# A fused short-convolution and mixture-of-experts layer: the order of the first loads and modulation, expert 0's loads, the search steps, expert 2's join and the last scatter

## The chip, the cores and the metric

The kernel runs on one core of one Trainium2 chip. Its time is in device microseconds (us), and a time given for a kernel is the median over its runs. TensorE (PE in the profile) multiplies, VectorE (DVE), ScalarE (ACT) and GpSimd (POOL) work element by element, and SyncE (SP) issues most DMAs. Each engine takes its instructions in the order in which they stand in the program.

## The reference, cut to what matters

One layer (DEPTH = 1, kind 0) over 2048 tokens of 1024 channels; all data are float32.

```python
m_l = (silu_c @ ada_w[i] + ada_b[i])[:, None, :]            # 1024 x 6144
sh1, sc1, g1, sh2, sc2, g2 = jnp.split(m_l, 6, axis=-1)
hl = modulate(rms_norm(lat, norm_g[i, 0]), sh1, sc1)        # x * (1 + scale) + shift
gate_b, gate_c, v = jnp.split(hl @ w_in, 3, axis=-1)        # 1024 x 3072
yl = (gate_b * dwconv_centred(gate_c * v, conv_w)) @ w_out  # 3 taps along the tokens
lat = lat + g1 * yl
h = modulate(rms_norm(lat, norm_g[i, 1]), sh2, sc2)
aff = jax.nn.softmax(h @ w_router, axis=-1)                 # 16 experts
g, idx = lax.top_k(jnp.swapaxes(aff, 1, 2), 256)            # each expert takes 256 tokens
hid = jax.nn.silu(xs @ w_gate) * (xs @ w_up)                # xs = h[idx]; 1024 x 1024 per expert
lat = lat + g2 * scatter_add(idx, (hid @ w_down) * g)
```

## The kernel before

**Products.** Each float32 operand is held as a rounded high part and the rest as a low part (fp32r), and a product is three matmuls: high by high, high by low, low by high. A piece of weights (512 KB) is loaded into a `raw` tile; ScalarE copies it to its high part (`split_high`, L212), VectorE subtracts to get the low part (`split_low`, L222), which frees the buffer and issues the next load. SP issues these loads (L196), in order.

**The head.** The four quarters of 512 tokens are `xq[q]`, four tiles of 128 rows each. `norm_x` scales the rows to unit norm: ScalarE sums the squares (L280), GpSimd makes 1/root of it in two small steps, VectorE multiplies (L393). `to_hl(q, k)` turns channel block k (128 channels) of a quarter on TensorE (four transposes, L398), applies scale `A1` and shift `sh1` on ScalarE twice, once rounded (L401) and once in full, and takes the low part on VectorE; the result is `hl[q, k]`. sh1 and A1 themselves are columns of `silu_c @ ada_w`: `load_ada_cols(k)` loads the 128 columns of block k for the shift and for the scale, with rows of 512 bytes; `ada_cols` lets VectorE sum the eight row blocks, weighted by `s_col`, into two accumulators `acc` of 256 columns (L429); `ada_sum` adds up the partitions by two matmuls of one column (`pcol`, L438), and `ada_fix` makes sh1 and A1 of it on VectorE.

`in_mm` is one step of `hl @ w_in`: nine matmuls of 512 columns (L451, L452, L454) into three banks, for the three channel blocks of gate_b, gate_c and v with the same number `ct`. Eight of them, k = 0 to 7, fill the banks, and `in_out` empties them. The loop of the head runs the pairs ct = 0 and ct = 1 of quarter 0 with a lag of three, `in_mm(pair[0], .., k)` beside `in_mm(pair[1], .., k - 3)`, so 16 in_mm in all; `norm_x(1, b)` stands at k = 6 and the eight `to_hl(1, j)` at k = 7 to 10. Then `constants()` (tables for the routing on GpSimd and VectorE) and the router's load follow, and the loop over `steps` takes up the remaining (ct, quarter) with eight in_mm each. Its first step, `steps[0]`, is quarter 1 with ct = 0.

**Routing and experts.** Which tokens an expert takes is found by a search for a threshold, in steps that are spread over other work: `tick(k)` runs the next step, in which TensorE's `pc` waits for ScalarE's count `hit` (L965 for L959). `pick_oh(e)` and `pick(e)` make the token numbers and issue two gathers `xs` on GpSimd (L1072); `fetch(0, i)` turns expert 0's rows (L1088), `turn` and `join` do it for the other experts. `gate_up(e, fh)` and `down(e, dh)` are the products (matmuls of 256 and of 512 columns), and after `down(e, 1)` two indirect DMAs on GpSimd add the result to the output (L1180). Behind `pick(0)` stand six matmuls `warm` (L1200), whose result nothing reads, and `split_to(first + 3)`, which splits expert 0's first four pieces and issues four more loads.

## Time and profile before

| what | value |
|---|---|
| median of 3 runs (lowest to highest) | 1913.16 us (1910.98 to 1913.17) |
| profiled execution, its own time | 1912.57 us |
| its span in the trace | 1910.8 us |
| its mean granted TensorE clock | 0.983 |
| PE busy | 1836.3 us, 96% of the span |
| DVE busy | 1136.9 us, 60% |
| ACT busy | 823.7 us, 43% |
| POOL busy | 304.4 us, 16% |
| HBM read, written | 300.51 MB, 50.33 MB |

The span is the time between the first and the last instruction or transfer in the trace of one execution; that execution's own time is 1.8 us longer. Busy times are means over stages with different limits: PE's 96% says that the kernel as a whole is bound by TensorE, and what is left to gain lies in the 74 us in which PE was not busy. A granted clock of 1.00 is TensorE's upper level, 2.4 GHz, and 0.50 the lower, 1.2 GHz.

### The profile page before, as it was taken

To read this page: it belongs to the slowest core of one execution; us is meant where nothing else is said; L and a number is where in the kernel's file an instruction comes from. 1 tells how busy PE (TensorE), PEld (TensorE's weight loads), DVE (VectorE), ACT (ScalarE), POOL (GpSimd) and SP (SyncE) were. 2 spreads that over 40 slices of the span, in tenths; PEclk is the share of its full clock that TensorE was granted. 3 is DMA by queue.
4 is the path that set the end of the run, shared out by engine and by line. 5 is a ranking of instruction groups with operands and counts; after the bars stand their busy time and mean duration, and the time that the engine had idled before them with its cause. 6 is when DMAs were issued, how large, how long until landed. Compare 5 with 4: busy or idle time off the path is not lost.

```text
span 1910.8 us, 29082 instructions
## 1 busy us (share of the span) xinstructions
PE 1836.3 (96%) x11568; PEld 1628.8 (85%) x11568; DVE 1136.9 (60%) x1633; ACT 823.7 (43%) x1046; POOL 304.4 (16%) x457
## 2 busy tenths in 40 slices
...
GB/s 281 145 113 146 77 160 61 105 137 143 72 72 190 259 257 257 134 219 201 214 249 216 242 248 249 231 227 266 220 239 236 258 219 241 255 238 236 221 231 89
DMA packets 308316, 375.30 MB, mean 196 GB/s; under 512 B 101788, under 2 KB 183764, under 8 KB 308180
## 3 DMA queue, kind: packets, MB, share of 16 engines
...
q14 instruction: 45, 0.37, 0.1%
HBM read 300.51 MB, written 50.33 MB: 184 GB/s over the span
## 4 chain that ended last, share of the span: by engine, by line
PE 89%; DVE 4%; DMA 3%; issue 1%; ACT 1%; POOL 1%; SPq 1%; POOLq 0%; DVEq 0%; ACTq 0%
PE pm L1131 12%; PE pm L1133 12%; PE pm L1135 12%; PE pm L451 9%; PE pm L452 9%; PE pm L454 9%; PE pm L1156 6%; PE pm L1154 6%; PE pm L1155 6%; PE pm L656 2%; PE pm L657 2%; PE pm L659 2%; DMA hl<-hl 1%; DMA xt<-in_x_dram 1%; PE pt L398 1%
## 5 line engine op out<-in xcount | busy, mean ns | idle before, releaser
L222 DVE TENSOR_TENSOR ws<-raw,ws 128x1024 fp32r<-128x1024 f32 x434 | 515.6, 1221 | 272.4 <-ACT ws L212 272.4
L212 ACT ACTIVATE ws<-raw 128x1024 fp32r<-128x1024 f32 x437 | 441.3, 1051 | 410.7 <-PE pm L1135 326.9
L1131 PE MATMUL pm<-xT,ws 128*128 128x256 f32 x2048 | 568.8, 278 | 0.0
L1133 PE MATMUL pm<-xT,ws 128*128 128x256 f32 x2048 | 567.1, 277 | 1.0 <-DVE xT L1111 0.9
L1135 PE MATMUL pm<-xT,ws 128*128 128x256 f32 x2048 | 566.8, 277 | 0.0
L1133 PEld LDWEIGHTS pm<-xT,ws 128*128 128x128 f32 x2048 | 385.9, 188 | 2.8 <-DVE xT L1111 1.1
L1131 PEld LDWEIGHTS pm<-xT,ws 128*128 128x128 f32 x2048 | 385.3, 188 | 1.7 <-ACT xT L1110 0.3
L1135 PEld LDWEIGHTS pm<-xT,ws 128*128 128x128 f32 x2048 | 385.2, 188 | 0.0
L451 PE MATMUL pm<-hl,ws 128*128 128x512 f32 x768 | 305.9, 398 | 1.0 <-ACT hl L401 1.0
L452 PE MATMUL pm<-hl,ws 128*128 128x512 f32 x768 | 302.0, 393 | 0.0
L454 PE MATMUL pm<-hl,ws 128*128 128x512 f32 x768 | 217.3, 391 | 0.0
L1180 POOL DMA_INDIRECT out_dram<-ot,idx x32 | 108.0, 3376 | 602.9 <-DVE ot L1174 598.8
L1156 PE MATMUL pm<-ws,hT 128*128 128x512 f32 x512 | 201.6, 394 | 0.0
L1154 PE MATMUL pm<-ws,hT 128*128 128x512 f32 x512 | 201.3, 393 | 0.0
L1155 PE MATMUL pm<-ws,hT 128*128 128x512 f32 x512 | 200.2, 391 | 0.0
L451 PEld LDWEIGHTS pm<-hl,ws 128*128 128x128 f32 x768 | 145.9, 190 | 31.9 <-ACT hl L401 1.4
L452 PEld LDWEIGHTS pm<-hl,ws 128*128 128x128 f32 x768 | 145.9, 190 | 30.5 <-issue 1.0
L454 PEld LDWEIGHTS pm<-hl,ws 128*128 128x128 f32 x768 | 145.5, 189 | 30.8
L461 ACT ACTIVATE cs<-pm 128x512 f32<-128x512 f32 x32 | 19.1, 598 | 332.1 <-issue 261.2
L464 DVE TENSOR_TENSOR u<-cs,pm 128x512 f32<-128x512 f32 x32 | 22.5, 703 | 231.3 <-ACT cs L461 231.3
L1156 PEld LDWEIGHTS pm<-ws,hT 128*128 128x128 f32 x512 | 96.2, 188 | 20.4
L1155 PEld LDWEIGHTS pm<-ws,hT 128*128 128x128 f32 x512 | 96.2, 188 | 20.2
(291 smaller groups left out, 1962.2 us busy)
## 6 DMA issues: line engine op xcount, KB each, us to landing
raw<-in_moe_w_gate_dram SPq DMA_DIRECT2D x128, 512.0 KB, 4.8
raw<-in_moe_w_up_dram SPq DMA_DIRECT2D x128, 512.0 KB, 4.2
raw<-in_moe_w_down_dram SPq DMA_DIRECT2D x128, 512.0 KB, 4.7
...
```

What stands on the lines that cost most here:

```text
L212: nc.scalar.activation(t[:, 0], raws[n_high], AF.Copy)
L222: (eng or nc.vector).tensor_sub(t[:, 1, ..., s], raw[..., s], t[:, 0, ..., s].bitcast(F32))
L451: nc.tensor.matmul(ps[m], wh, t[:, 0], start=(k == 0), stop=False)
L452: nc.tensor.matmul(ps[m], wl, t[:, 0], start=False, stop=False)
L454: nc.tensor.matmul(ps[m], W(k, m)[0], t[:, 1], start=False, stop=(k == KD - 1))
L1131: nc.tensor.matmul(o, w[:, 0, j, c0], xT[:, 0, k], start=(k == 0 and f % 2 == 0), stop=False, skip_group_check=True)
L1133: nc.tensor.matmul(o, w[:, 0, j, c0], xT[:, 1, k], start=False, stop=False, skip_group_check=True)
L1135: nc.tensor.matmul(o, w[:, 1, j, c0], xT[:, 0, k], start=False, stop=(k == KD - 1), skip_group_check=True)
L1154: nc.tensor.matmul(ps[s], h, w[:, 0, j], start=(k == 0), stop=False)
L1155: nc.tensor.matmul(ps[s], h, w[:, 1, j], start=False, stop=False)
L1156: nc.tensor.matmul(ps[s], l, w[:, 0, j], start=False, stop=(k == KD - 1))
L1180: st = nc.gpsimd.indirect_dma_start(out=out_rows, out_offset=bass.IndirectOffsetOnAxis(ap=idx_of[e][:, s:s + 1], axis=0), in_=ots[s], in_o ...
```

## The change

In the **head**, quarter 0 of x loads first. ada_w's columns come in four groups of two channel blocks, 256 columns a piece (rows of 1 KB), and w_in's columns of ct = 0 and 1 come together, in four parts by rows, in the same order (`load_w`, `high_w`, `low_w`). The weighted sum has one accumulator of 512 columns; its first product is ScalarE's in groups 1 to 3, and in group 0 TensorE takes the first three row blocks itself, multiplied by `s_col` (`ada_mm`). `ada_fix` runs on ScalarE. `wake(n)` issues transposes that nothing reads. Both pairs run side by side, without a lag, two k in a group. The squares of quarter 0 are shared between ScalarE and VectorE. Quarter 1's norms stand in the last group, its first three `to_hl` there and behind it, and the other five inside steps[0]. `constants()`, the router's rows and the start values of `cnts` move into the loop over steps.

At **expert 0**, `split_to(first + 3)` issues its four loads from GpSimd (`load_by`), behind the gathers, and 14, 8 and 3 warm matmuls stand where six stood. The **search steps** (`tick`) skip the k at which TensorE's order now has something else, and **expert 2's** turn and join come one k and one place earlier. The **last scatter** (expert 15) goes in five parts: two halves after `down(15, 0)`, then a half and two quarters, the quarters as products of their own with 256 columns (`last_down`, `scatter_part`).

```diff
+    load_by = [nc.sync]
...
-        nc.sync.dma_start(t, dram(src, offset, ap))
+        load_by[0].dma_start(t, dram(src, offset, ap))
...
+        def to_hl(q, k):
+            turn_x(q, k)
+            low_x(q, k, scale_x(q, k))
...
+        groups = [(0, 2), (2, 2), (4, 2), (6, 2)]
+
+        def load_ada_cols(g):
+
+
+            k0, n = groups[g]
+            ada_t[g] = []
+            for r in range(0, KD, 2):
+                t = hl_tile([P, 2, 2, n * P], F32)
+                ada_t[g].append(t)
+                for j in range(2):
+                    nc.sync.dma_start(t[:, j], dram(ada_w, (r + j) * P * 6 * D + k0 * P,
+                                                    [[6 * D, P], [D, 2], [1, n * P]]))
...
+        def ada_cols(g, r0, r1):
+
             for r in range(r0, r1):
+                if g not in ada_a:
+                    ada_a[g] = m2("acc")
+                    if g:
+                        nc.scalar.activation(ada_a[g], ada_row(g, r), AF.Copy, scale=s_col[:, r:r + 1])
+                    else:
+                        nc.vector.tensor_scalar(ada_a[g], ada_row(g, r), s_col[:, r:r + 1], None, op0=ALU.mult)
                 else:
+                    nc.vector.scalar_tensor_tensor(ada_a[g], ada_row(g, r), s_col[:, r:r + 1], ada_a[g],
+                                                   op0=ALU.mult, op1=ALU.add)
             if r1 == KD:
+                ada_t.pop(g)
...
+        def ada_mm(g, v, col):
+            n, new = groups[g][1], g not in pcols
+            if new:
+                pcols[g] = tp.tile([P, 2, n], F32, name="pcol", tag="tp")
             for h in range(2):
+                for j in range(n):
+                    c0 = (n * h + j) * P
+                    nc.tensor.matmul(pcols[g][:, h, j:j + 1], v[:, c0:c0 + P], col, start=(new and h + j == 0),
+                                     stop=True, skip_group_check=True)
+
+        def ada_sum(g):
+            ada_mm(g, ada_a.pop(g), ones_f[:, 0:1])
+
+        def ada_fix(g, j):
+            k = groups[g][0] + j
+            s = slice(k, k + 1)
+            nc.scalar.activation(sh1[:, s], pcols[g][:, 0, j:j + 1], AF.Identity, bias=bsh_col[:, s])
+            nc.scalar.activation(A1[:, s], pcols[g][:, 1, j:j + 1], AF.Identity, bias=A0[:, s], scale=g0_col[:, s])
...
+            if ps_ == 0 and ct < 2:
+                return lambda k, m: tuple(w_pair[m, k // 4][:, j, k % 4, ct * P:(ct + 1) * P] for j in range(2))
...
+        def load_w(g):
+            for m in range(3):
+                if g == 0:
+                    w_raw[m, 0] = wpool.tile([P, 4, 2 * P], F32, name="raw", tag="raw", bufs=n_raw)
+                elif g == 2:
+                    w_raw[m, 1] = hl_tile([P, 4, 2 * P], F32) if m else b4("rb", [P, 4, 2 * P])
+                nc.sync.dma_start(w_raw[m, g // 2][:, 2 * (g % 2):2 * (g % 2) + 2],
+                                  dram(w_in, 2 * g * P * 3 * D + m * D, [[3 * D, P], [3 * D * P, 2], [1, 2 * P]]))
...
+        def wake(n):
+            t = mm.tile([P, QT], F32, name="pm", tag="mm")
+            for i in range(n):
+                nc.tensor.transpose(t[:, 0:P], xq[0][0][:, 0:P], identf)
+
+        def mm_pair(i, k):
+            in_mm(pair[i], 0, W_chan(0, i), k)
...
+        load_x(0)
         load_ada_cols(0)
+        load_w(0)
         load_ada_cols(1)
+        load_w(1)
+        vrow, nr = row_cols("v_row", [(ada_b, 0, 16), (norm_g, 0, 8), (conv, 0, 24)], nc.gpsimd)
+        rs = [rstd_of(xq[0][b], m2("sq", D, BF) if b % 2 else junk, nc.vector if b % 2 else None) for b in range(3)]
+        norm_x(0, 0, nc.scalar, rs[0])
+        rs.append(rstd_of(xq[0][3], m2("sq", D, BF), nc.vector))
+        norm_x(0, 1, nc.scalar, rs[1])
+        for b in range(2, 4):
+            norm_x(0, b, None, rs[b])
         vcols = to_cols("v_col", vrow, nr)
         bsh_col, bsc_col, g0_col = vcols[:, 0:8], vcols[:, 8:16], vcols[:, 16:24]
         cw = [vcols[:, 24 + 8 * i:32 + 8 * i] for i in range(3)]
+        A0 = consts.tile([P, 8], F32, name="A0")
+        nc.vector.scalar_tensor_tensor(A0, bsc_col, 1.0, g0_col, op0=ALU.add, op1=ALU.mult)
+        for r in range(3):
+            ada_mm(0, ada_row(0, r), s_col[:, r:r + 1])
+        turn_x(0, 0)
+        ada_cols(0, 3, KD)
+        wake(12)
+        ada_sum(0)
+        high_w(0)
+        for m in range(3):
+            low_w(0, m)
+        wake(8)
         pair = [new_banks() for _ in range(2)]
+        for g in range(4):
+            k = 2 * g
+            more_g = g < 3
+            ada_fix(g, 0)
+            full = scale_x(0, k)
+            ada_fix(g, 1)
+            if g:
+                low_w(g, 1)
+                low_w(g, 2)
+            if more_g:
+                ada_cols(g + 1, 0, 1)
+            low_x(0, k, full)
+            mm_pair(0, k)
+            turn_x(0, k + 1)
+            full = scale_x(0, k + 1)
+            if more_g:
+                ada_cols(g + 1, 1, 5)
+            low_x(0, k + 1, full)
+            mm_pair(1, k)
+            if more_g:
+                turn_x(0, k + 2)
+                high_w(g + 1)
+                ada_cols(g + 1, 5, KD)
+            else:
+                rs = [rstd_of(xq[1][b], junk) for b in range(4)]
                 for b in range(4):
+                    norm_x(1, b, None, rs[b])
+            mm_pair(0, k + 1)
+            if g < 2:
+                load_ada_cols(g + 2)
+                load_w(g + 2)
+            if g == 1:
+                load_x(1)
+            if more_g:
+                ada_sum(g + 1)
+                low_w(g + 1, 0)
+            else:
                 in_out(pair[0], 0, 0)
+                to_hl(1, 0)
+            mm_pair(1, k + 1)
+        to_hl(1, 1)
+        to_hl(1, 2)
+        load_end[0] = len(pieces)
+        load_to(n_done + n_raw - 1)
         pend = (pair[1], 0, 1)
...
+                if (ps_, ct, q) == (0, 0, 1) and k + 3 < KD:
+                    to_hl(1, k + 3)
...
+            if i == 3:
+                before, ones_b, tri, slot_r, step, bias, need, zero1, cnts, aux, same, quick = constants(m2)
+                nc.sync.dma_start(rt, dram(router, 0, [[E, P], [E * P, KD], [1, E]]))
+                nc.scalar.activation(rts[:, :, 0], rt, AF.Copy)
+                nc.vector.tensor_sub(rts[:, :, 1], rt, rts[:, :, 0].bitcast(F32))
...
+    def last_down(ps, product):
+
+        ots = ot_of[E - 1]
+
+        def finish(s, o, c0, n):
+            nc.vector.scalar_tensor_tensor(ots[s][:, c0:c0 + n], o, gate_of[E - 1][:, s:s + 1], g2b[:, c0:c0 + n],
+                                           op0=ALU.mult, op1=ALU.mult)
+            scatter_part(s, c0, n)
+
+        for k in range(KD):
+            product(0, k)
+        finish(0, ps[0], H, H)
+        for i in range(2):
+            c = slice(i * CAP, (i + 1) * CAP)
+            o = mm.tile([P, CAP], F32, name="pm", tag="mm")
+            for k in range(KD):
+                w, j, t = ws_of[w_moe[2, E - 1, 1, k // 2]], k % 2, slice(P, 2 * P)
+                h, l = (hT_of[E - 1][k // 4][:, n, k % 4, t] for n in range(2))
+                nc.tensor.matmul(o, h, w[:, 0, j, c], start=(k == 0), stop=False)
+                nc.tensor.matmul(o, h, w[:, 1, j, c], start=False, stop=False)
+                nc.tensor.matmul(o, l, w[:, 0, j, c], start=False, stop=(k == KD - 1))
+            finish(1, o, H + i * CAP, CAP)
...
+        if (e, dh) == (E - 1, 0):
+            index_parts([(0, 0, H), (1, 0, H)])
+            index_parts([(0, H, H), (1, H, CAP), (1, H + CAP, CAP)])
+            for s in range(2):
+                scatter_part(s, 0, H)
...
-    for i in range(6):
-        nc.tensor.matmul(warm, same, ws_of[first][:, 0, 0], start=(i == 0), stop=(i == 6 - 1))
+
+    def keep_warm(n):
+        for i in range(n):
+            nc.tensor.matmul(warm, same, ws_of[first][:, 0, 0], start=(i == 0), stop=(i == n - 1))
+
+    keep_warm(14)
+    split_high(first + 4)
+    load_by[0] = nc.gpsimd
     split_to(first + 3)
+    load_by[0] = nc.sync
     for i in (0, 2, 1, 3):
         fetch(0, i, mm)
+        if i > 1:
+            keep_warm(8 if i == 2 else 3)
     for e in range(E):
         if e == 0:
             gate_up(0, 0, lambda k: pick_oh(1) if k == 1 else pick(1) if k == 3 else
                     (tick(k), turn(1, 0) if k == 7 else None) if k in (2, 4, 5, 6, 7) else None)
             gate_up(0, 1, lambda k: join(1, k // 2 - 2) if k in (4, 6) else
-                    (tick(k), turn(1, 1) if k == 1 else None) if k < 4 else None)
+                    turn(1, 1) if k == 1 else tick(k) if k in (0, 2, 3, 5) else None)
             continue
         if e == 1:
-            gate_up(1, 0, lambda k: tick(k) if k else None)
+            gate_up(1, 0, lambda k: tick(k) if k not in (0, 2) else None)
             down(0, 0, tick)
             for _ in rounds:
                 pass
             pick_oh(2)
-            gate_up(1, 1, lambda k: pick(2) if k == 1 else turn(2, k - 5) if k in (5, 6) else None)
+            gate_up(1, 1, lambda k: pick(2) if k == 1 else turn(2, k - 4) if k in (4, 5) else
+                    join(2, 0) if k == 7 else None)
```

Where instructions stand now, at three places. First SP's queue at the start of the program, as it was before; `raw` with 128x4x128 is half a piece of w_in for ct = 0:

```order
L75 DMA c_row<-in_c_dram 8x128
L414 DMA hl<-in_ada_w_dram 128x4x128 x4
L384 DMA xt<-in_x_dram 128x1024 x4
L75 DMA v_row<-in_ada_b_dram 16x128
L75 DMA v_row<-in_norm_g_dram 8x128
L75 DMA v_row<-in_sc_conv_dram 24x128
L240 DMA raw<-in_sc_w_in_dram 128x4x128 x3
L414 DMA hl<-in_ada_w_dram 128x4x128 x4
L240 DMA raw<-in_sc_w_in_dram 128x4x128 x3
L414 DMA hl<-in_ada_w_dram 128x4x128 x4
L196 DMA raw<-in_sc_w_in_dram 128x8x128 x3
L414 DMA hl<-in_ada_w_dram 128x4x128 x20
```

And SP's queue at the same place in the change:

```order
L75 DMA c_row<-in_c_dram 8x128
L363 DMA xt<-in_x_dram 128x1024 x4
L407 DMA hl<-in_ada_w_dram 128x2x256 x8
L535 DMA raw<-in_sc_w_in_dram 128x2x256 x3
L407 DMA hl<-in_ada_w_dram 128x2x256 x8
L535 DMA raw<-in_sc_w_in_dram 128x2x256 x3
L407 DMA hl<-in_ada_w_dram 128x2x256 x8
L535 DMA rb<-in_sc_w_in_dram 128x2x256
L535 DMA hl<-in_sc_w_in_dram 128x2x256 x2
L407 DMA hl<-in_ada_w_dram 128x2x256 x8
```

x moved ahead of ada_w, each group's ada_w and w_in alternate, and the small `v_row` loads left this queue.

Second TensorE around quarter 1's first transposes. Before, they stood behind an in_mm of pair[1] whose operand `hl_407` had long been made, with another such in_mm behind them (`xt_467` to `xt_473` are quarter 1's tiles):

```order
L454 MATMUL pm_203<-hl_407,ws_296 128x512
L454 MATMUL pm_204<-hl_407,ws_332 128x512
L454 MATMUL pm_205<-hl_407,ws_335 128x512
L398 MATMUL pt_627<-identf_79,xt_467 128x128
L398 MATMUL pt_627<-identf_79,xt_469 128x128
L398 MATMUL pt_627<-identf_79,xt_471 128x128
L398 MATMUL pt_627<-identf_79,xt_473 128x128
```

In the change they stand between in_mm(0, 7) and in_mm(1, 7), the last two of the four groups (`xt_437` to `xt_443` are quarter 1's tiles):

```order
L458 MATMUL pm_252<-hl_566,ws_404 128x512
L458 MATMUL pm_253<-hl_566,ws_406 128x512
L458 MATMUL pm_254<-hl_566,ws_408 128x512
L379 MATMUL pt_625<-identf_79,xt_437 128x128
L379 MATMUL pt_625<-identf_79,xt_439 128x128
L379 MATMUL pt_625<-identf_79,xt_441 128x128
L379 MATMUL pt_625<-identf_79,xt_443 128x128
L455 MATMUL pm_255<-hl_566,ws_404 128x512
```

Both of those in_mm read `hl_566`, the last block of quarter 0; the transposes moved from four in_mm ahead of the end of the pairs to one ahead of it.

Third GpSimd's queue from expert 0's gathers on, before:

```order
L824 CAST aux<-ex 128x16
L1072 DMA xs<-hscr,idx 128x1024 x2
L1072 DMA xs<-hhalf,idx 128x2048 x4
L1180 DMA out_dram<-ot,idx 2048x1024
L1179 MEMSET spacer 1x1
```

And in the change:

```order
L884 CAST aux<-ex 128x16
L1132 DMA xs<-hscr,idx 128x1024 x2
L196 DMA raw<-in_moe_w_up_dram 128x2x512
L196 DMA raw<-in_moe_w_gate_dram 128x2x512
L196 DMA raw<-in_moe_w_up_dram 128x2x512
L196 DMA raw<-in_moe_w_gate_dram 128x2x512
L1132 DMA xs<-hhalf,idx 128x2048 x4
L1288 DMA out_dram<-ot,idx 2048x1024
```

Four weight loads, which SP issued, now stand on GpSimd's queue behind expert 0's two gathers.

## Rows read from the trace of the kernel before

**Rows 1.** Windows: from:to, length, busy us (PE PEld DVE ACT POOL), PEclk, DMA, GB/s.

```profile
19.59:51.81 32.22, 20.14 (x69) 15.35 (x70) 30.65 (x62) 11.14 (x15) 12.28 (x7) 0.74 1.16 300
...
78.36:100.99 22.63, 22.63 (x110) 18.79 (x109) 10.70 (x30) 9.50 (x16) 8.42 (x79) 1.00 0.04 13
100.99:780.00 679.01, 676.49 (x3177) 557.41 (x3175) 334.82 (x447) 220.17 (x298) 105.03 (x238) 1.00 0.49 149
...
798.00:836.70 38.70, 15.38 (x66) 11.84 (x67) 27.57 (x117) 18.59 (x42) 3.34 (x2) 0.50 0.42 150
836.70:1901.96 1065.26, 1061.01 (x7935) 993.08 (x7934) 691.55 (x884) 535.20 (x625) 149.50 (x77) 1.00 0.77 230
```

**Rows 2.** Waits of PE from 0 to 101 us: total us, times, longest.

```profile
PE pcol L438 <- DVE acc L431: 19.1, 5, 7.0
```

**Rows 3.** Timeline of PE in the head: start us, length us, engine, line, operation.

```profile
36.12 0.63 PE L451 MATMUL pm<-hl,ws 128*128 128x512 f32 x1
36.55 0.63 PE L452 MATMUL pm<-hl,ws 128*128 128x512 f32 x1
...
80.52 1.03 PE L398 MATMUL pt<-identf,xt 128*128 128x128 f32 x8
...
98.79 0.39 PE L451 MATMUL pm<-hl,ws 128*128 128x512 f32 x1
...
100.15 0.84 PE L454 MATMUL pm<-hl,ws 128*128 128x512 f32 x3
100.83 0.39 PE L451 MATMUL pm<-hl,ws 128*128 128x512 f32 x1
```

**Rows 4.** DMA from 0 to 120 us, in 40 slices of 3 us.

```profile
GB/s 5 255 319 405 321 291 290 290 286 294 292 291 288 287 294 290 359 394 205 0 0 38 283 320 326 250 99 6 0 0 0 0 0 0 95 87 106 290 336 145
```

**Rows 5.** Groups by form, 0 to 101 us: busy us, mean ns, idle before.

```profile
L401 ACT ACTIVATE hl<-pt,sh,A 128x512 fp32r<-128x512 f32 x16 | 12.5, 780 | 31.9 <-PE pt L398 21.1 <-DVE A L445 7.8 <-issue 2.9
L250 ACT ACTIVATE ws<-raw 128x512 fp32r<-128x512 f32 x6 | 3.8, 628 | 1.9 <-DMA raw<-in_sc_w_in_dram 1.8
L469 DVE SCALAR_TENSOR_TENSOR y<-u,v_col,y 128x512 f32<-128x512 f32 x2 | 1.5, 751 | 1.8 <-ACT y L468 1.8
L251 DVE TENSOR_TENSOR ws<-raw,ws 128x512 fp32r<-128x512 f32 x2 | 1.3, 678 | 0.0
```

**Rows 6.** Timeline of quarter 1's norms: first square, last norm.

```profile
66.22 1.05 ACT L280 ACTIVATE junk<-xt 128x1024 bf16<-128x1024 f32 x1
...
73.05 0.75 DVE L393 TENSOR_SCALAR xt<-xt,rstd 128x1024 f32<-128x1024 f32 x1 [0.71 <-POOL rstd L283]
```

**Rows 7.** Expert 0's gathers `xs`: PE's waits, timeline, issue to landing us.

```profile
PE pt L1088 <- DMA xs<-hscr,idx: 6.6, 2, 4.1
...
822.55 1.80 POOL L1072 DMA_INDIRECT xs<-hscr,idx  x1 [0.30 <-issue]
...
824.69 0.37 SPq L196 DMA_DIRECT2D raw<-in_moe_w_gate_dram  x1
...
830.77 0.48 PE L1088 MATMUL pt<-identf,xs 128*128 128x128 f32 x1 [2.48 <-DMA xs<-hscr,idx]
...
DMA to landing us min/median/max: 5.6/7.4/9.1
```

**Rows 8.** Waits of PE from 836.7 to 1000 us: total us, times, longest.

```profile
PE pc L965 <- ACT hit L959: 2.5, 2, 1.3
PE pm L1133 <- DVE xT L1111: 0.9, 1, 0.9
```

**Rows 9.** The end: timeline; GB/s in 40 slices of 0.21 us from 1902.5 us.

```profile
1901.56 0.40 PE L1156 MATMUL pm<-ws,hT 128*128 128x512 f32 x1
...
1903.02 1.57 POOL L1180 DMA_INDIRECT out_dram<-ot,idx  x1 [3.91 <-DVE ot L1174]
...
GB/s 158 20 0 0 0 0 0 0 0 0 0 0 118 197 0 59 138 178 118 158 217 197 178 257 197 178 257 59 20 0 0 0 0 0 0 0 0 0 0 0
```

**Rows 10.** The scatters: issue ns min/median/max, first and last start.

```profile
L1180 POOL DMA_INDIRECT out_dram<-ot,idx x32: 1552/1620/5977, 957.8 to 1903.0; - x32
```

192 lines of the change are left out of this document (62 added, 130 removed).

## Prediction

> **What bounds the kernel now.** I read the table of stretches first [rows 1]. TensorE is busy in 676.5 of 679.0 us from 101 to 780 us and in 1061.0 of 1065.3 us from 836.7 us to its last matmul; there nothing but its own work sets the end, and the change leaves that work alone. TensorE loses time in three places: the head up to 101 us (20.1 of 32.2 us busy from 19.6 to 51.8), the routing (15.4 of 38.7 us from 798 to 836.7), and what comes behind the last matmul.
>
> In the head its waits [rows 2] name one thing: five waits, 19.1 us together, of `pcol` (ada_sum) for `acc`, VectorE's sums over ada_w's rows. The timeline [rows 3] gives the rest. At 36.1 us a matmul of 512 columns starts 0.43 us behind the one before it (the lower level, 1.2 GHz; the granted clock is 0.74 in this stretch), so that one `in_mm`, 9 matmuls, takes 3.85 us. At 99 us one in_mm starts 2.04 us behind the other (2.4 GHz). The 24th in_mm, the last of steps[0], ends at 100.99 us: the mark against which I measure the head. The DMA row [rows 4] shows loads at about 290 GB/s from 15 to 45 us, where nearly all have rows of 512 bytes (128 columns), and some 400 GB/s where x's 4 KB rows move.
>
> **The change part by part.**
>
> *Head, start.* x (2.1 MB), group 0 of ada_w (2.1 MB) and its share of w_in (0.8 MB) come first. The flow begins near 3 us [rows 4]; x at 400 GB/s takes 5.2 us; the other 2.9 MB have 1 KB rows, whose rate no row shows: at 290 and 400 GB/s they take 10.0 and 7.2 us, and I take 350 (8.3), since 1 KB lies between the two. So w_in's part lands near 17 us. A copy to high parts (0.63), the fix on ScalarE and the scaling (0.78) follow [rows 5]: the first in_mm starts between 18 and 21 us. I take 19.6, which happens to be its start before.
>
> *Head, the four groups.* TensorE's work to the end of the 16th in_mm: 16 x 2.04 = 32.6; seven sets of four transposes at 0.5 (eight take 1.03 [rows 3]), 3.5; three sums of four one-column matmuls, an estimate of 0.35 each, under a set of transposes. That is 37.1 us, some 9.7 in a group. VectorE's work in a group: three low parts of weights and two of hl at 0.68, seven sums of 512 columns at 0.75 [rows 5]: 3.4 + 5.3 = 8.7 us, less than TensorE's. ScalarE's: three copies and a product at 0.63, four scalings at 0.78, four small ones at about 0.2: 6.4. A group's loads (2.9 MB) take 8.3 us at 350 GB/s and 10 at 290; even at 290 the last of w_in lands at 3 + 5.2 + 39.7 = 48 us, before group 3 starts (19.6 + 2.7 + 3 x 9.7 = 51). So TensorE becomes the bound, and the rate matters little. Its clock: before, the first four in_mm ran at the lower level, 1.8 us longer each. Behind the 20 transposes of wake() I take one and a half of them, 2.7 us (bounds 0 and 7.2). Group 3's work would then end at 19.6 + 37.1 + 2.7 = 59.4 us.
>
> *Head, x of quarter 1.* Here the change adds a wait. ScalarE squares the four tiles of quarter 1 behind scale_x(0, 7), and TensorE has to_hl(1, 0), which needs all four, ahead of the 16th in_mm. Before, the chain from the first square (66.22) to the end of the last norm (73.05 + 0.75) took 7.6 us [rows 6], GpSimd's small steps and VectorE's norms in turn, and stood beside in_mm that did not need it. From the end of turn_x(0, 7): 1.55 of scaling + 7.6 = 9.1 us, and TensorE has two in_mm to do meanwhile, 4.1. It waits 5.0 us; in_mm(1, 7), the next transposes, and in_out(pair[0]), which must empty the banks that steps[0] writes, are queued behind.
>
> *Head, sum.* 59.4 + 5.0 + 1.5 (three sets of transposes) + steps[0] with eight in_mm and five sets (18.8) = 84.7; 1.3 for a fall of the clock in that wait (bounds 0 and 3.5: the in_mm and three sets behind it at half speed) gives 86.0. Against 100.99: **-15.0** (bounds: -9, with all four low-clock in_mm and waits for VectorE of half a us in each group, and -20, with the new wait hidden).
>
> On that wait the Trainium skill (TensorE: Matmul & The Clock Gate, "HAM oscillation") says that a TensorE that waits for data between bursts goes back to the lower clock and starts each burst slow. By it the fall costs the full 3.5, and the head would gain 12.8. The granted 0.74 of [rows 1], where TensorE waited again and again, agrees with the rule's direction.
>
> *Constants, router rows, cnts.* They move into steps 3 and 5, into the stretch in which TensorE is busy 676.5 of 679.0 us and VectorE 335; nothing waits for them before 798 us: 0. Without that cover the bound is the 8.4 us that GpSimd was busy from 78 to 101 us [rows 1].
>
> *Expert 0.* In the routing TensorE waits 6.6 us for the two gathers `xs` [rows 7]. The second is issued from 822.55 to 824.35 and used first at 830.77; four weight loads of 512 KB, the last issued at 824.69 by SP, run beside it. They now stand behind both gathers on GpSimd's queue. The fastest gather took 5.6 us from issue to landing [rows 7]; so would the second, landing at 828.2, 2.5 us earlier (bounds 0 and 3). The clock: until 836.7 us it was granted 0.50 [rows 1], so of some four us of gate_up's matmuls two are lost. 14 + 8 + 3 warm matmuls are to keep it up; but the 8 stand ahead of fetch(0, 1), and at the lower level they take 8 x 0.43 = 3.4 us and eat the earlier gather. Between a gain of 4.5 and one of 0 I take **-3.5**.
>
> *Ticks and expert 2's join.* Two waits of `pc` for ScalarE's hit counts, 2.5 us, and one of 0.9 for expert 2's xT [rows 8]. Ticks next to them are skipped, and join(2, 0) comes a step earlier: of 3.4 us I take **-2.0** (bounds -3.4 and +1, if a wait only moves to another tick).
>
> *Last scatter.* Behind the last matmul (ends 1901.96): VectorE's product of 512 columns (0.75 us by the like of it in [rows 5]), the issue from 1903.02 to 1904.59, data until about 1908.7, the end at 1910.8 [rows 9]. The last piece is now a quarter, 128 x 256: VectorE 0.4, the same issue, and 0.9 of data for 3.5. TensorE's work is the same in matmuls of 256 columns, which gate_up uses throughout. **-2.9** (bounds -3.2, and -1.5 if the issues of the last three pieces queue up on GpSimd).
>
> *Sum.* -15.0 - 3.5 - 2.0 - 2.9 = -23.4: a span of 1887.4 for 1910.8. The profiled execution took 1912.57, so 1889.2; the median of the runs is 0.6 above it, and I say **1889.5 us**. Its own range, from bounds that can go together, is 1884 to 1895 us.
>
> **The rivals.** Less than 0.2% (3.8 us) is about what a measurement of this kernel can't tell from no change.
>
> *The clock stays low through the groups.* If hand-offs leave holes in each group, twelve of the 16 in_mm run at 3.85 us: 22 us more, of which 2.7 are counted; in return the wait for quarter 1 shrinks by 3.6 and no clock is left to fall (1.3). About +14: 1904. For it: before, four in_mm in 32 us ran so. Against: the groups have 9.7 us of TensorE's work in 9.7. 0.10.
>
> *VectorE's sums still end last.* If its 8.7 us stretch to 13 by waits for ScalarE, three groups wait 4 us each, like the five waits of before: 1901.5. Against: seven sums of 512 columns do what 18 instructions of 256 did. 0.07.
>
> *The four loads starve on GpSimd.* Its indirect issues took 1.62 us at the median and up to 5.98 [rows 10]. Four at 6.0 from 824.4 us end at 848.4; the fourth lands some 4 us later and its split ends near 855, where gate_up's second half, 22 us behind the first, wants it at about 851; with the load before it TensorE would wait some 8 us: 1897.5. Nearest row: the median. 0.08. The Trainium skill (SBUF — State Buffer, "SBUF: two separate sides") speaks for this rival: the descriptors of a DMA that GpSimd issues are written by GpSimd itself, some VectorE instructions shut it out of the port for that, and the page advises against that queue beside them.
>
> *All goes well.* No fall of the clock, the wait hidden, the gathers' full 4.5: 1883. 0.12.
>
> *Slower than before.* The mechanism is the head's loads. The other parts gain 8.4, so it turns slower if the head ends after 109.4: group 3 then begins near 74 us, and w_in's last part (13.6 MB in all) lands at 72, under 200 GB/s on the way. No steady slice of these loads shows less than 286 [rows 4]. 0.03. *No difference*: the groups wait as long as before and the rest moves within its bounds. 0.02.
>
> **How the numbers follow.** The main case has 0.58, the rivals what is given. Faster by over 0.2%: 0.95; within: 0.02; slower: 0.03. The range for 8 in 10 takes the main case, the starving loads and the good case: 1883 to 1898.
>
> **What would show it.** The 24th in_mm ends at 86 us (under 82 or over 92, and the head's term is wrong). Waits of `pcol` for `acc` fall from 19.1 us to under 3; a wait of about 5 us of quarter 1's transposes for VectorE's norm appears near 60 us. The granted clock is 1.00 from 25 us on but for a dip behind that wait. gate_up(0, 0) starts 2 to 3 us earlier as seen from pick(0), at 2.4 GHz, and 6 us lie behind the last matmul. The prediction fails if matmuls run 0.43 us apart beyond 30 us, or if quarter 1's transposes don't wait.

## The result and the profile after

The changed kernel takes 1897.13 us (median of 5 runs, 1896.77 to 1903.16) where the kernel before takes 1913.0 in the same comparison: ratio 0.9928, 95% interval 0.9914 to 0.9942. That is faster, as forecast, but by less than the 23.7 us that were forecast: 1897.13 lies 7.6 us above 1889.5 and 0.9 below the end of the range, and the ratio times the median shown before (0.9928 x 1913.16 = 1899.4) lies 1.4 beyond that end. A third or more of the forecast gain did not come. The five runs of the changed kernel lie up to 6.4 us apart, so that a difference of some 2 us between two profiled executions says little by itself. The profiled execution took 1897.13 us, its span is 1895.3 and its mean granted clock 0.990.

The table of stretches of the kernel after (columns as in [rows 1], to which it answers):

```profile
22.70:61.38 38.68, 38.52 (x189) 31.06 (x187) 27.07 (x39) 22.75 (x46) 1.00 (x3) 1.00 0.98 307
61.38:66.13 4.75, 1.12 (x5) 0.55 (x5) 2.61 (x5) 2.51 (x5) 3.46 (x7) 0.93 0.70 242
66.13:69.73 3.60, 3.60 (x12) 2.84 (x13) 2.68 (x6) 2.06 (x3) 0.00 (x0) 0.61 0.00 0
69.73:89.34 19.61, 19.61 (x102) 16.35 (x100) 8.11 (x13) 11.21 (x17) 2.27 (x6) 1.00 0.07 28
89.34:577.32 487.98, 487.98 (x2170) 401.06 (x2168) 201.41 (x270) 115.48 (x156) 61.44 (x203) 1.00 0.35 112
577.32:786.50 209.18, 201.93 (x1087) 166.05 (x1087) 147.82 (x223) 111.79 (x160) 56.80 (x126) 0.99 0.80 230
```

The reader is to see three things. From the first in_mm (22.70) to the end of the 15th (61.38) TensorE now stands still for 0.16 us, where [rows 1] had 12 us of holes in 19.59 to 51.81. Then comes a hole, 61.38 to 66.13, and behind it a stretch at a granted clock of 0.61. And the stretch from the last in_mm (577.32) to the search's first `pS` (786.50) takes 209.18 us for the same 1087 matmuls that took this in the kernel before:

```profile
588.98:796.03 207.05, 200.39 (x1087) 165.40 (x1086) 147.55 (x223) 111.51 (x160) 56.23 (x126) 1.00 0.82 233
```

So something was given back in a stage whose work the change leaves alone. The waits of TensorE up to 90 us, after ([rows 2] had 19.1 us for `acc`):

```profile
PE prow L81 <- DMA v_row<-in_sc_conv_dram: 5.3, 1, 5.3
PE pt L379 <- DVE xt L372: 3.6, 4, 1.1
PE prow L81 <- DMA c_row<-in_c_dram: 2.9, 1, 2.9
PE pcol L437 <- DMA hl<-in_ada_w_dram: 1.9, 1, 1.9
```

The waits for `acc` are gone; quarter 1's transposes wait for VectorE's norms. The timeline of TensorE ahead of the first in_mm, after ([rows 3]):

```profile
10.97 5.25 PE L437 MATMUL pcol<-s_col,hl 128*128 128x1 f32 x24 [1.94 <-DMA hl<-in_ada_w_dram]
16.09 1.09 PE L379 MATMUL pt<-identf,xt 128*128 128x128 f32 x4
16.97 2.77 PE L555 MATMUL pm<-identf,xt 128*128 128x128 f32 x12
19.53 1.71 PE L437 MATMUL pcol<-ones_f,acc 128*128 128x1 f32 x8
21.10 1.95 PE L555 MATMUL pm<-identf,xt 128*128 128x128 f32 x8
22.70 0.78 PE L455 MATMUL pm<-hl,ws 128*128 128x512 f32 x1
```

TensorE's own queue fills this: the 12 one-column matmuls of `ada_mm`, each of which the trace shows as two records of 0.22 us, so 24; four transposes; the 12 transposes of `wake(12)`; and the sum of group 0 (four such matmuls, eight records), all in turn. The sum starts at 19.53, though VectorE's `acc`, which it adds up, is done at 17.85.

Marks read from the timelines (matmul ends and starts) cut every kernel into the same stages. "Head" ends with the 24th in_mm, "in_mm" with the 256th, "routing" with the first `pS`, "search" with the start of `pick(0)`'s last `pi`, "expert 0" with gate_up(0, 0), "ticks" with gate_up(2, 0), "steady" with the last matmul, and "tail" is what lies behind it. Times in us of the profiled executions:

| kernel | first in_mm | head ends | in_mm | routing | search | expert 0 | ticks | steady | tail |
|---|---|---|---|---|---|---|---|---|---|
| before | 19.59 | 100.99 | 487.99 | 207.05 | 23.26 | 38.80 | 119.30 | 924.57 | 8.84 |
| after | 22.70 | 89.34 | 487.97 | 209.18 | 23.53 | 34.85 | 119.49 | 924.46 | 6.48 |
| difference | +3.11 | -11.65 | -0.02 | +2.13 | +0.27 | -3.95 | +0.19 | -0.11 | -2.36 |
| rest_only | 20.51 | 100.62 | 487.98 | 207.50 | 23.27 | 34.64 | 118.47 | 924.46 | 6.76 |
| x1late | 20.91 | 87.27 | 487.94 | 211.40 | 23.54 | 35.18 | 118.55 | 924.46 | 6.76 |
| wake | 20.83 | 87.45 | 487.97 | 212.45 | 23.52 | 34.87 | 121.32 | 924.46 | 6.75 |
| x1early | 21.55 | 82.54 | 487.97 | 210.33 | 23.53 | 34.67 | 121.31 | 924.46 | 6.70 |
| tile_only | 20.67 | 83.55 | 502.94 | 212.83 | 23.60 | 35.27 | 121.43 | 924.46 | 6.72 |

The differences from the head's on add up to -15.5, the difference of the spans.

### The profile page after: what moved, and what is told of

It is laid out like the page before. It is cut to its first block, busy times and chain, and to the rows that moved or that the text cites. A ratio compares the mean times of both kernels' runs of the same rounds, so it can differ in the third digit from the quotient of the medians.

```text
span 1895.3 us, 29225 instructions
## 1 busy us (share of the span) xinstructions
PE 1843.0 (97%) x11655; PEld 1636.0 (86%) x11655; DVE 1122.3 (59%) x1586; ACT 829.4 (44%) x1066; POOL 295.6 (16%) x459
## 4 chain that ended last, share of the span: by engine, by line
PE 86%; DVE 4%; DMA 2%; issue 2%; ACT 2%; SPq 0%; POOL 0%; POOLq 0%; DVEq 0%; ACTq 0%
PE pm L1191 12%; PE pm L1193 12%; PE pm L1195 12%; PE pm L455 8%; PE pm L456 8%; PE pm L458 8%; PE pm L1260 6%; PE pm L1258 6%; PE pm L1259 6%; PE pm L716 2%; PE pm L719 2%; PE pm L717 2%; DMA xt<-in_x_dram 1%; DVE ws L222 1%; PE pt L379 1%
## 5 line engine op out<-in xcount | busy, mean ns | idle before, releaser
L1260 PE MATMUL pm<-ws,hT 128*128 128x512 f32 x504 | 198.4, 394 | 0.0
L1258 PE MATMUL pm<-ws,hT 128*128 128x512 f32 x504 | 198.3, 393 | 0.0
L1259 PE MATMUL pm<-ws,hT 128*128 128x512 f32 x504 | 197.1, 391 | 0.0
L465 ACT ACTIVATE cs<-pm 128x512 f32<-128x512 f32 x32 | 19.1, 598 | 316.7 <-issue 234.9
```

The source lines that it names most:

```text
L1258: nc.tensor.matmul(ps[s], h, w[:, 0, j], start=(k == 0), stop=False)
L1259: nc.tensor.matmul(ps[s], h, w[:, 1, j], start=False, stop=False)
L1260: nc.tensor.matmul(ps[s], l, w[:, 0, j], start=False, stop=(k == KD - 1))
```

## The experiments

**Theories.** The main one has two parts. The shortfall in the head is the chain to the first in_mm and the wait for quarter 1; the 2 us in the routing come from the head's new length, which shifts TensorE's fetches of its own code against the loads of `vscr` (the gated product, which `out_split` loads back from DRAM and ScalarE copies to its high part, L645 before, L705 after). The rivals: the routing's loss comes from what was moved into the loop over steps, or from the new order itself; and the waits in the head hide one behind the other, so that removing one gives nothing.

**rest_only**: the kernel before, with the change at expert 0, the search steps, expert 2's join and the last scatter, and the old head.

> The kernel before with the parts at expert 0, the search steps, expert 2's join and the last scatter, without the new head and without the moved constants. Theory: the parts add up, and these are worth +3.9 (expert 0), -0.2 (search steps and join) and +2.3 (tail): 6.0 us, some 1907.0. The stage of the router then takes what it takes in other runs of before. Rival (the new head costs 2.1 us in the router's stage): 6.0 here as well, but 207.0 us in that stage here and 209 in every kernel with the new head. Rival (the parts at the experts only work behind the new head): under 4 us.

Measured: 1905.6 us (7 runs), ratio 0.9968 (0.9956 to 0.9979). The routing takes 207.50, as before; a second profile of the kernel before (before_again, one run, 1911.12 us) has 207.41. So the tail and expert 0 bring some 6 us by themselves, and the routing's loss comes with the new head or with what moved into the loop, both of which are left out here.

**x1late**: quarter 1's first transposes one in_mm later.

```diff
-                to_hl(1, 0)
             mm_pair(1, k + 1)
+        to_hl(1, 0)
```

> The change with quarter 1's first transposes behind the 16th in_mm, in place of ahead of it. In the change TensorE ends the 15th at 61.38 and starts the 16th at 66.13, and runs that at half rate (3.60 us). Theory (TensorE waits in order for the last norm, and the wait drops its clock): the 16th fills 2.0 of the wait at full rate, the transposes still wait until about 66, and the 24th in_mm ends 2.0 to 3.3 us earlier, at 86.0 to 87.3. Rival (the wait only moves: steps[0] needs the last norm anyway, and the clock falls in the shorter wait too): the gain is 2.0 less what the slower transposes and in_mm lose, 0.5 to 1 us, at 88.3 to 88.8.

Measured: 1900.66 us (4 runs), 0.9943 (0.9926 to 0.9959). From the end of the 15th in_mm to the head's end it takes 28.11 us, after 27.96: nothing gained, and the theory falls here (that the head ends at 87.27, inside its forecast, is due to the start at 20.91). Its timeline behind the 16th in_mm:

```profile
64.42 0.72 ACT L472 ACTIVATE y<-u,v_col 128x512 f32<-128x512 f32 x1 [2.66 <-DVE u L468]
65.05 0.76 ACT L384 ACTIVATE hl<-pt,sh,A 128x512 fp32r<-128x512 f32 x1
...
66.53 1.11 PE L379 MATMUL pt<-identf,xt 128*128 128x128 f32 x4 [1.98 <-ACT full L385]
```

Now in_out's product `y` stands ahead of the scaling on ScalarE, waits 2.66 us for VectorE's `u`, which stands behind the norms, and TensorE waits for the scaling. The late thing is the chain of norms; moving its user only chooses the queue in which the wait stands.

**x1early**: the chain starts earlier instead. The squares of tiles 0 and 1 go to the end of group 2, those of tiles 2 and 3 behind ada_fix in group 3, and the norms follow the low parts there.

```diff
+            if g == 3:
+                rs += [rstd_of(xq[1][b], junk) for b in range(2, 4)]
...
+            for b in range(2, 4 if g == 3 else 2):
+                norm_x(1, b, None, rs[b])
...
+                if g == 2:
+                    rs = [rstd_of(xq[1][b], junk) for b in range(2)]
```

> The change with quarter 1's norms earlier: the squares of two tiles at the end of the third group and of two at the start of the fourth, the norms between the low parts there; the order of the transposes is the change's. From the end of the 15th in_mm to that of the 24th the change takes 27.96 us (29.40 in two kernels with the same head), and moving the transposes behind the 16th in_mm left 28.11. Theory (the last norm, at 65.94, sets the start of the 16th, and the wait for it drops the clock): the chain ends before the 15th in_mm does, no wait and no fall are left, and the stretch takes 22.3 to 24.5. Rival 1 (in_out of the first pair stands ahead of quarter 1's scaling on ScalarE and its banks are those that steps[0] writes, so the wait only moves there): 25.5 to 27. Rival 2 (the squares delay ScalarE in the groups): the 15th in_mm ends over 1 us later as counted from the first one's start (38.68 in the change).

Measured: 1891.63 us (4 runs, 1890.41 to 1893.32), 0.9885 (0.987 to 0.99). This version beats both kernels and has the lowest median of the study. The stretches from the end of the 15th in_mm, of x1early:

```profile
59.81:62.33 2.52, 2.52 (x15) 2.08 (x14) 1.23 (x2) 1.71 (x4) 0.00 (x0) 1.00 0.90 309
62.33:82.54 20.21, 19.84 (x102) 16.34 (x100) 9.74 (x17) 11.87 (x19) 2.84 (x6) 1.00 0.11 43
```

No hole, no fall of the clock, 22.73 us instead of 27.96: the wait and what follows from it were worth 5.2 us.

Part of that is lost again: its ticks take 121.31 us, 1.8 more than after, with the same instructions. The place is expert 2's start, behind two waits for its turned rows (0.8 and 0.9 us), first after, then x1early:

```profile
942.50:946.10 3.60, 3.60 (x32) 3.60 (x33) 3.60 (x4) 2.41 (x3) 0.00 (x0) 1.00 0.45 141
```
```profile
936.98:940.58 3.60, 3.60 (x19) 3.60 (x19) 3.60 (x4) 2.28 (x3) 0.00 (x0) 0.53 0.53 167
```

The granted clock falls to 0.53, and 19 matmuls run where after has 32. The same fall stands in wake, best3, tile_only and sp_loads, whose ticks take 121.2 to 122.0 us.

**wake**: `wake(12)` removed.

> The change without the 12 transposes of wake ahead of the first sum over partitions (the other 8 stay behind it). Theory: VectorE's acc of group 0 is done at 17.85, but TensorE's sum of it starts at 19.53, behind those transposes; fix, scaling and in_mm follow it in a chain of 3.2 us. Without them the first in_mm starts at 21.0 to 21.4 in place of 22.70 and the 24th ends 1.3 to 1.7 earlier, near 87.8. Rival (the transposes bring the clock up): more in_mm run at half rate, 1.8 us longer each; with one more the gain is gone, with two the 24th ends at 91.

Measured: 1900.34 us (4 runs), 0.9942 (0.9925 to 0.9958). From the end of VectorE's `acc` to the first in_mm it takes 3.38 us instead of 4.84, so the 12 transposes cost 1.5 on that chain in after; with them gone the sum waits 0.77 us for `acc`, so the 24 records ahead of them are not what it waits for. But x1late, which has the transposes, needs 3.42 us for the same chain. There the sum takes 0.95 us, where it took 1.71 in after and 1.86 in wake:

```profile
18.55 0.95 PE L437 MATMUL pcol<-ones_f,acc 128*128 128x1 f32 x8
```

Behind it the matmuls of the first in_mm start 0.23 us apart from the second on in x1late, while in after the first four start 0.43 or more apart. That is TensorE at half its speed, although the granted clock is shown as 1.00 for both. So the transposes pay for themselves in some executions and not in others. The six kernels with the changed kernel's whole head have their first in_mm between 21.0 and 23.0, and the routing of wake (212.45) took more than its start gave: some 10 us into it the granted clock is 0.66 over 5 us, in x1late too.

**sp_loads** (expert 0's four loads back on SP), **warm6** (six warm matmuls, as before) and **old_ticks** (before's places of the search steps), each alone:

```diff
-    load_by[0] = nc.gpsimd
...
-    load_by[0] = nc.sync
```
```diff
-    keep_warm(14)
+    keep_warm(6)
...
-        if i > 1:
-            keep_warm(8 if i == 2 else 3)
```
```diff
-                    turn(1, 1) if k == 1 else tick(k) if k in (0, 2, 3, 5) else None)
+                    (tick(k), turn(1, 1) if k == 1 else None) if k < 4 else None)
...
-            gate_up(1, 0, lambda k: tick(k) if k not in (0, 2) else None)
+            gate_up(1, 0, lambda k: tick(k) if k else None)
```

> The change with expert 0's four loads issued by SP again, nothing else undone. From the last matmul of pick(0) to the end of gate_up(0, 0) the kernels of before take 38.65 to 38.80 us, the change 34.85, rest_only 34.64. Theory (the four loads run beside the second gather and delay it by 2 to 2.5 us; the warm matmuls hold the clock, worth the rest): 36.5 to 37.4. Rival 1 (the warm matmuls are all of it): 34.9. Rival 2 (both are needed, since the clock falls in the longer wait): 38.5.

> The change with 6 warm matmuls behind pick(0) and none between the fetches, as before. Theory (the clock is half of the gain at expert 0): gate_up(0, 0) starts at the same place but at half rate for some 4 us, so that the stretch from pick(0) to its end takes 36.5 to 37 in place of 34.85. Rival 1 (the earlier gathers alone keep the clock up): 34.6 to 34.9, or less, since 11 matmuls fall away. Rival 2 (the 8 between the fetches cost what they bring): 34.9 to 35.5 with a slow start but an earlier last fetch.

> The change with the search steps where they stood before, expert 2's turn and join as in the change. From the end of gate_up(0, 0) to that of gate_up(2, 0) the kernels of before take 118.60 and 119.30 us, the change 119.49, others with its steps 118.5 to 119.0 where the clock does not fall. Theory (a skipped step is made up later, so that the search ends later and pick(2) waits for VectorE instead): the two waits of pc of 1.2 us each come back, the waits of pick(2) go, and the stretch takes 118.3 to 119.3. Rival 1 (the new places gain the 2 us that was forecast, and the earlier join loses them): 120.5 or more. Rival 2 (the old places are better): 117.5 or less.

Measured, one run and one profile each: 1902.58, 1900.56 and 1897.1 us; their expert 0 took 37.06, 36.62 and 35.00, after 34.85. So the order of the loads is worth 2.2 us and the warm matmuls 1.8. The first stretch of gate_up(0, 0), after, warm6 and before:

```profile
821.24:825.40 4.16, 4.01 (x34) 3.73 (x33) 4.16 (x5) 3.21 (x4) 0.00 (x0) 1.00 0.73 264
```
```profile
821.86:826.00 4.14, 4.00 (x20) 3.70 (x20) 3.98 (x5) 3.55 (x4) 0.00 (x0) 0.56 0.66 256
```
```profile
832.57:836.70 4.13, 3.99 (x18) 3.69 (x18) 3.71 (x5) 3.92 (x5) 0.00 (x0) 0.50 0.08 9
```

34 matmuls against 20 and 18 in the same time: that is the clock. The ticks of old_ticks take 119.09 us, after 119.49; where the clock does not fall, that stage lies between 118.5 and 120.2 in all kernels. TensorE's waits there, first after, then old_ticks:

```profile
PE pm L1193 <- DVE xT L1171: 1.7, 2, 0.9
PE pi L1121 <- DVE oh L1113: 1.3, 4, 0.3
PE pm L1191 <- ACT xT L1170: 0.6, 1, 0.6
...
PE pc L1025 <- ACT hit L1019: 0.4, 1, 0.4
```
```profile
PE pc L1025 <- ACT hit L1019: 2.1, 2, 1.2
PE pm L1193 <- DVE xT L1171: 0.9, 1, 0.9
```

The wait for the hit counts did go, 2.1 to 0.4, and came back as waits for expert 2's turned rows and for `oh`, since the search ends later and pick(2) stands close behind it.

**after_shift, before_shift, before_shift2**: 64, 48 and 36 matmuls of one column whose result nothing reads, early in the head, which move all later code of TensorE by as many places (and add the tile `zb` that they read).

```diff
+        zb = m2("zb", P, BF)
+        nc.gpsimd.memset(zb, 0.0)
+        dummy = mm.tile([P, QT], F32, name="pm", tag="mm")
+        for i in range(64):
+            nc.tensor.matmul(dummy[:, 0:1], zb, zb[:, 0:1], start=True, stop=True, skip_group_check=True)
```

> The change with 64 more matmuls of one column (and 64 weight loads) on TensorE while it waits for the first data; nothing reads their result. From the last in_mm to pS (the router's stage) before, its second trace and rest_only take 207.05 to 207.50 us, the three kernels with the new head 209.18, 211.40 and 212.45. In these three a 16 KB fetch on the instruction queue starts 8 to 11.5 us ahead of the last in_mm's end, where w_out's last loads and the first loads of vscr run; in the other three it starts 31 us ahead and 2 us behind. Theory (that fetch shares DMA engines with the vscr loads, which land some 0.6 us late, TensorE waits for them, and the chain behind keeps late): the extra instructions move the fetch by half of its period, to 20 to 25 us ahead, and the stage takes 207.3 within 0.5. Rival 1 (the new head slows the stage by something else, buffers or moved constants): 209 to 213 as before the shift. Rival 2 (the clock at the start): the head's end moves too, by over 1 us, but the stage does not.

> The kernel before with 48 such matmuls of one column at the start, where TensorE waits for the first data. They move the 16 KB fetch that stands 2 us behind the last in_mm to some 9 us ahead of it, where it stands in the kernels with the new head. Theory (the fetch delays the vscr loads): the router's stage takes 208.3 to 212 us in place of 207.05 to 207.50, the head changes little. Rival (it is the new head or the moved constants): 207.0 to 207.5.

> The kernel before with 36 matmuls of one column at the start. With 48 the code fetch fell 12.4 us ahead of the last in_mm's end, and the router's stage took 207.93 us against 207.05 to 207.50. With 36 it should fall 6 to 9 us ahead, beside the vscr loads themselves. Theory (the fetch delays them): 208.3 to 212. Rival (the new head slows that stage by something else; 207.93 was within the scatter): 207.0 to 207.6.

Measured: 1900.52 (4 runs), 1913.74 (10 runs, ratio 1.0012, 1.0002 to 1.0022) and 1913.24 us (one run). The routing: 207.85, 207.93 and 209.98. after_shift's head ends 4 us later, 3.2 of them because the first of these matmuls waits for GpSimd's zeroing until 13.38 us. The DMA view of the 12 us ahead of the last in_mm's end, in a second profile of the kernel before (routing 207.41) and in before_shift2 (209.98), queue, packets, MB, share:

```profile
q1 hardware_dynamic: 2512, 2.62, 72.2%
q0 software_dynamic: 80, 0.26, 5.9%
q14 instruction: 1, 0.01, 0.2%
```
```profile
q1 hardware_dynamic: 2509, 2.62, 75.2%
q0 software_dynamic: 80, 0.26, 6.3%
q8 instruction: 1, 0.02, 0.6%
q14 instruction: 1, 0.01, 0.2%
```

In before_shift2 a block of TensorE's code (q8; it moves with the extra matmuls) comes in 1.6 us ahead of the first issue for `vscr`, beside the last loads of w_out. ScalarE's copy of what `vscr` brings, in the kernel before and in before_shift2 (last in_mm's end: 588.98 and 587.63), starts 1.66 and 0.85 us ahead of the last in_mm's end:

```profile
587.32 1.06 ACT L645 ACTIVATE hl<-hl 128x1024 fp32r<-128x1024 f32 x1 [9.81 <-DMA hl<-vscr]
```
```profile
586.78 1.06 ACT L650 ACTIVATE hl<-hl 128x1024 fp32r<-128x1024 f32 x1 [10.62 <-DMA hl<-vscr]
```

With the old head and nothing but these extra matmuls and their tile, the routing takes 209.98 where the block falls 9.4 us ahead of that end; in after it falls 11.3 us ahead. The Trainium skill (Runtime: NRT & Kernel Launch, "Instruction fetch mechanics") says that code comes in blocks of 16 KiB by a DMA queue of the engine's own and that the cost of a block's boundary is mostly hidden. The blocks are there in the trace; here one beside other loads went with a copy that starts 0.8 us later against the mark, against that "hidden", in one execution. But its position doesn't settle the 2 us: with 48 matmuls the block falls 12.4 us ahead and the routing takes 207.93.

Nor does most of the loss arise at the mark. The routing has the same matmuls in all kernels, so each can be timed from the last in_mm's end. Two of them, in the kernel before (588.98) and in old_pad (575.68; described below, it has the changed kernel's code but for one tile's size):

```profile
595.65 1.96 PE L843 MATMUL pl<-rt,st 128*128 128x16 f32 x16 [0.25 <-ACT st L840]
...
766.76 0.66 PE L739 MATMUL pt<-identf,u 128*128 128x128 f32 x4 [0.17 <-DVE hl L744]
```
```profile
582.25 1.96 PE L903 MATMUL pl<-rt,st 128*128 128x16 f32 x16 [0.25 <-ACT st L900]
...
755.22 0.66 PE L799 MATMUL pt<-identf,u 128*128 128x128 f32 x4 [0.91 <-DVE hl L804]
```

The first starts 6.67 us behind the mark in the kernel before, 7.12 in after, 7.49 in before_shift2 and 6.57 in old_pad; the second 177.8, 179.3, 180.7 and 179.5. So old_pad, with no delay at the mark, loses 1.8 us all the same (208.83), and after has 0.45 us there of its 2.13. Another half us of after's is the clock at the end: in the last 5 us of the routing it is granted 0.58, where the kernel before has 0.97.

**best3 and best4**: x1early without `wake(12)`, and that with 64 such matmuls that read the constant `identf`, so that no tile is added.

> The change with quarter 1's norms early and without the 12 transposes ahead of the first sum; no matmuls added. Theory (both edits add up): the first in_mm starts near 21 us, the 24th ends at 81 to 82.5 (x1early: 82.54 with its start at 21.55). The code fetch then falls some 8 us ahead of the last in_mm's end, as in the kernel without the 12 transposes, so the router's stage takes 210 to 212.5, and the profiled execution 1890.5 to 1893. Matmuls of the middle stand 226.7 ns apart. Rival (the kernel with all three edits was slow through one of these two): 234 ns apart, 1906 or more.

> The same with the 64 matmuls of one column at the start, which read the identity matrix and no tile of their own. In the kernel with three edits (its matmuls read a tile of the pool m2, zeroed by VectorE) all matmuls of 512 columns up to the experts stood 234.3 ns apart in place of 226.7, and the middle took 15 us more. Theory for that (the extra tile shifts the tiles that in_out and the groups take from m2, the matmuls as such do no harm): 226.7 ns here, the fetch falls 20 to 25 us ahead of the last in_mm's end, the router's stage takes 207.5 to 208.3, the execution 1887 to 1890. Rival (the extra instructions on TensorE do it): 234 ns, 1905 or more.

Measured (4 runs each): 1895.5 (0.9916, 0.9899 to 0.9932) and 1892.46 us (0.99, 0.9884 to 0.9917). The routing: 210.94 and 209.20. Moving the block from 7.6 to 22.2 us ahead of the mark went with 1.7 us less, but not with the 207.3 of the kernel before: if the fetch is a cause, it is not the only one. Neither version beats x1early, so no gain shows from removing wake(12).

**best2 and tile_only**: x1early without wake(12), with the zeroed tile `zb` of the shift experiments, and with (best2) or without (tile_only) the 64 matmuls.

> The change with three edits: no 12 transposes ahead of the first sum, quarter 1's norms early, and 64 matmuls of one column at the start that move the code fetch out of the way of the first vscr loads. Theory: the head ends at 82 to 84 us in place of 89.34, the router's stage takes 207.9 in place of 209.2 to 212.5, the rest is the change's: a profiled execution of 1888 to 1892. Rival (the stages behind take back what the head gives, as the router's did): the head ends as early, but the time stays at 1894 to 1897.

> The first of these kernels with the extra tile of m2, zeroed by VectorE, and no matmuls that read it. Theory (the extra tile shifts the others): 234 ns between matmuls of the middle, 1906 or more. Rival (the instructions): 226.7 ns and the time of the first of these kernels.

Measured: 1911.25 (11 runs, ratio 0.9992) and 1912.59 us (one run). All of the gain is lost in the in_mm stretch: 502.96 and 502.94 us instead of 487.97, without any wait. The tile does it, not the matmuls (best4 has them without the tile, and 487.99). The same tile, asked for later in the program, did no harm in after_shift (487.98). Groups of in_mm's second matmul from 200 to 560 us, in tile_only and, as the normal case, old_pad (below):

```profile
L456 PE MATMUL pm<-hl,ws 128*128 128x512 f32 x496 | 196.6, 396 | 0.0
```
```profile
L456 PE MATMUL pm<-hl,ws 128*128 128x512 f32 x512 | 199.4, 389 | 0.0
```

496 instead of 512 of them fit into the same 360 us: one starts some 234 ns behind the other instead of 227, from start to start in the timeline.

**aligned_tile, old_pad, ws_off**: where the tiles lie. aligned_tile is tile_only with 32 bytes more, which put `hl` back on a multiple of 64 bytes by the compiled program; old_pad is the changed kernel with the pad tile of the kernel before (64 bytes); ws_off is old_pad with a tile of 32 bytes that moves only what comes behind it.

```diff
+        mix.tile([P, 8], F32, name="fill", tag="fill", bufs=1)
```

> The kernel with the extra tile (x1early, without the 12 transposes, with the tile of m2 at the start; 1912.59 us, 234 ns between matmuls) and 32 bytes more in the pool mix behind that tile. In the compiled programs the tiles hl, which TensorE streams in in_mm, begin at addresses that are multiples of 64 in all kernels with 226.7 ns, and 32 bytes behind one in the two with 234 ns. Theory (that address makes the stream 3% slower): with the 32 bytes hl begins at multiples of 64 again, 226.7 ns, 1890 to 1895 us. Rival (the extra tile changes which buffers wait for which): 234 ns, 1912.

> The change with one line undone: the tile pad of the pool consts has its old 64 bytes in place of 32. All tiles behind it (hl, ws, xT, hT) then begin 32 bytes behind a multiple of 64. Theory (the streamed operand's address counts): matmuls of 512 columns 234 ns apart in the middle, 15 us more there, and more in the experts too, whose streamed tiles xT and ws are moved as well: 3% of gate_up's and down's time would be some 28 us, so 1912 to 1942 in all. Rival (only DMA or other engines care): 1896 to 1902.

> The same with 32 bytes more in the pool mix, so that hl begins at multiples of 64 and ws, xT and hT do not. Theory (only the streamed operand counts, not the one that is loaded as weights): in_mm, which streams hl and loads ws, stays at 226.7 ns and the middle at 488.0 us; the output projection and down, which stream ws, and gate_up, which streams xT, are slower by 2 to 3%. Rival (any operand off the multiple of 64 slows a matmul): 234 ns in in_mm as well.

Measured, one run each: 1910.46, 1895.31 and 1914.85 us; in_mm 501.09, 487.97 and 500.99. If the tiles lie as the expectations say (no view here shows addresses), hl's own place does not decide: on a multiple of 64 bytes it is slow in aligned_tile and ws_off, off it it is fast in old_pad. ws_off needs neither `zb` nor any extra instruction. And the changed pad line shows no worth by itself.

## Why the prediction was right or wrong

Three terms of the sum failed: "Head, start", "Ticks and expert 2's join", and the routing, which the prediction put at nothing. What it named as signs came: the waits for `acc` went, quarter 1's wait and the dip of the clock behind it appeared, and 6.48 us lie behind the last matmul.

- **Head, -15.0 forecast, -11.65 measured.** The step that failed is "Head, start": the first in_mm at 19.6. It starts at 22.70, +3.1 of the 3.35 that are missing. In the six kernels with this head it starts at 22.1 in the mean, +2.5, and the head ends at 87.7 to 90.9, mean 89.4, so the shortfall is no accident of one execution. I followed the arrival of w_in's part, which was right (its copies begin at 16.88), and not the sum of group 0, on which `ada_fix` and the scaling wait: VectorE's `acc` ends at 17.85, wake's transposes stand ahead of the sum until 19.5, and the sum takes 1.71 us (0.95 where TensorE was fast by then), for which the start had no term. The rest held, in part by luck: 15 in_mm of the groups took 38.68 us (39.8 less one in_mm of 2.04, 37.8, forecast), without holes, so neither VectorE nor the loads were the bound; but the three later sums took 1.02 us each where I had 0.35, and the slow matmuls at the start cost under 1 us where I had 2.7; the wait for quarter 1 was 4.75 (5.0), and what came behind it 23.21 (2.04 + 1.5 + 18.8 + 1.3 = 23.6).
- **The fall of the clock.** In 66.13 to 69.73 it is 0.61, for 1.1 us by x1early's 2.52 at 1.00 (the 16th in_mm takes 3.6 to 4.2 us in the six kernels, so 1.1 to 1.7). I chose 1.3 between 0 and 3.5. The Trainium skill's rule (TensorE: Matmul & The Clock Gate, "HAM oscillation"), by which I gave 12.8 for the head, agrees in direction; here the fall ended after one in_mm.
- **Constants, router rows: 0.** Right: 487.97 against 487.99 us.
- **Expert 0, -3.5: measured -3.95.** Right, by both of its means: 2.2 from the order of the loads, 1.8 from the clock. The four issues on GpSimd took 0.75 to 0.81 us each, so the rival of starving loads did not come, and the Trainium skill's rule that stands beside it in the prediction (SBUF — State Buffer, "SBUF: two separate sides") shows no cost here:

```profile
813.30 1.79 POOL L1132 DMA_INDIRECT xs<-hscr,idx  x1 [0.30 <-DVE ws L222]
815.09 0.81 POOL L196 DMA_DIRECT2D raw<-in_moe_w_up_dram  x1
...
817.31 0.75 POOL L196 DMA_DIRECT2D raw<-in_moe_w_gate_dram  x1
```

- **Ticks and join, -2.0: measured +0.19.** Wrong. The wait I counted did shrink, but its bound "if a wait only moves to another tick" is what happened; old_ticks, at 119.09, shows no worth in the new places.
- **Tail, -2.9: measured -2.36**; -2.0 to -2.4 over all kernels with it. The end, after:

```profile
1888.55 0.28 PE L1249 MATMUL pm<-ws,hT 128*128 128x256 f32 x1
1888.86 0.48 DVE L1234 SCALAR_TENSOR_TENSOR ot<-pm,gate,g2b 128x256 f32<-128x256 f32 x1 [2.24 <-PE pm L1249]
1889.62 1.56 POOL L1222 DMA_INDIRECT out_dram<-ot,tbits  x1 [1.12 <-DVE ot L1234]
```

- **Routing and search, no term: measured +2.13 and +0.27.** The largest thing that I had no term for: "the change leaves that work alone" was true of the instructions and not of their time. What the runs show, from one profiled execution each (two of the kernel before): the kernel before and rest_only have 207.05 to 207.50, the eleven kernels with the new head and in_mm at its usual pace 207.85 (after_shift) to 212.45 (wake). Moving TensorE's code went with more (before_shift2) and with less (after_shift, best4). After's loss is made up of 0.45 us at the mark, some 1.1 between that and 182 us (half of it a longer wait for the low part `hl`), and 0.56 in the last 5 us with the lower clock. The cause stays open: why 36 extra matmuls raise it and 48 do not, why old_pad loses the time with no delay at the mark, and why x1early, best3 and best4 stay at 209 or more.

Together the misses are 3.35 in the head, 2.4 in the routing and search, 2.2 in the ticks and 0.5 in the tail, less 0.45 at expert 0 and 0.1 in the steady part: 7.9 us, the whole distance from -23.4 to -15.5. (The forecast's last step has a slip: 1889.2 and 0.6 make 1889.8, not 1889.5.)
